# Wide half-precision products with no reader, set among the float32 products of a recurrence

## The chip, the cores and the metric

The kernel runs on one core of a Trainium2 chip. The metric is the time of one execution on the device, in microseconds. A core has a matrix engine (TensorE, PE in the profile, with its weight loads listed apart as PEld), a vector engine (VectorE, DVE), a scalar engine (ScalarE, ACT), GpSimd (POOL) and SyncE (SP), which here issues most of the transfers. Each works through its own list of instructions in order, and they wait for one another by semaphores. TensorE reads its operands from the on-chip memory and writes sums to PSUM, which has eight banks per partition; one bank holds 512 float32 values per partition.

## The reference

The reference is one layer of a hybrid decoder. A prompt of 2048 tokens and eight short samples of 8 tokens go through one input projection; its columns feed four groups of heads: attention, a gated linear recurrence, an RWKV-7 recurrence and a diagonal state-space model. Their outputs are joined, gated, projected by `w_out`, normalized and added to the input. What matters here is the RWKV-7 group, whose state goes from token to token, and the output projection:

```python
def step(S, inp):
    r_t, w_t, k_t, v_t, kk_t, a_t = inp
    sa = jnp.einsum('bhij,bhj->bhi', S, -kk_t)
    S = (S * w_t[:, :, None, :] + sa[..., None] * (kk_t * a_t)[:, :, None, :]
         + v_t[..., None] * k_t[:, :, None, :])
    return S, jnp.einsum('bhij,bhj->bhi', S, r_t)
...
y = x + rms_norm(jnp.einsum('bte,ed->btd', o, w_out), norm_post)
```

## The kernel before

The first 1180 us or so are projections, attention, the linear recurrence and the state-space model; the change does not touch them. Then comes the last phase, in `program` from line 1865 on: the RWKV-7 recurrence over sixteen blocks of 128 tokens (`rw_prompt`), the recurrence of the samples beside it (`rw_sample`), and the output projection tile by tile (`out_prep`, `out_tile`).

A block goes through these steps. `rw_prep` makes its vectors. `rw_mats` makes its matrices, on PSUM tiles named ra. `rw_base` solves the 16 by 16 diagonal pieces for two blocks at once: fifteen products of the tile r_de into ra, and then thirty short steps on VectorE (lines 1280 and 1281), in which each step needs the one before. `rw_tri` joins the pieces to the inverse of 64 by 64 (tiles r_XY, r_M, r_H, r_NA, on PSUM tiles rl). `rw_chain` carries the state through two chunks (tiles r_gs, r_Z, r_BK, r_ET, on PSUM tiles rc), and `rw_norm` normalizes. All these products are in float32, mostly 64 or 128 columns wide, and go through the small class `Marked` (`self.PE`), which hands them to TensorE and notes them in a list `done` that nothing reads. `front(i + 3)` runs up to three blocks ahead of the chain.

`out_tile` is the output projection of a tile of 128 tokens: two groups (g) of 24 float16 products of 512 columns each, the weights of the product being a piece of the tile's activations (o_h) and the moving operand a piece of `w_out` held as float16 (the tile wo, loaded once, lines 1537 and 1538). A group sums in one PSUM tile named acc; `ACB = 2` gives acc two banks, so that the next group may start while ScalarE (line 1612) still reads the one before. Products of `out_tile` are tied behind certain products of the chain (`spine`), so that they come among them.

The order on each engine is not written by hand: a scheduler of the framework puts the instructions in order by its own estimate of when each can run, within the bounds of the data and of `issue_after`, which keeps an instruction behind another on its engine. So a product that is added can also move the others.

Of the kernel before, what the change touches and what calls it, by code (L numbers as in the profile page):

```python
# [13 lines left out]
F32 = mybir.dt.float32  # L14
# [9 lines left out]
P = 128  # L24
# [12 lines left out]
class Marked:  # L37


    def __init__(self, eng):  # L40
        self.eng, self.done = eng, []

    def matmul(self, *a, **k):
        r = self.eng.matmul(*a, **k)  # L44
        self.done.append(r.ins)
        return r

    def transpose(self, *a, **k):
        r = self.eng.transpose(*a, **k)
        self.done.append(r.ins)  # L50
        return r


class Part:


    def __init__(self, ctx, tc, ins, outs):
        self.ctx, self.tc, self.nc = ctx, tc, tc.nc
        self.i, self.o = ins, outs
        nc = self.nc  # L60
        self.PE = Marked(nc.tensor)
        self.cst = ctx.enter_context(tc.tile_pool(name="cst", bufs=1))
        self.dram = ctx.enter_context(tc.tile_pool(name="scr", bufs=1, space=DRAM))
        self.od = [self.dram.tile([P, KT, n], F32, name=f"od{b}") for b, (_, n) in enumerate(BLK)]
        self.opool, self.gated, self.prep, self.wos = None, {}, {}, True
        self.onext = self.npiece = self.rwi = 0
        self.ident = self.cst.tile([P, P], F32, name="ident")
        make_identity(nc, self.ident)
        self.ones1 = self.cst.tile([1, P], F32, name="ones1")
        nc.vector.memset(self.ones1, 1.0)  # L70
        self.onec = self.cst.tile([P, 1], F32, name="onec")
        nc.vector.memset(self.onec, 1.0)
        self.vec = self.cst.tile([P, NVEC], F32, name="vec")
        nc.sync.dma_start(self.vec, ins["vec"])
# [1517 lines left out]
    def out_tile(self, i, h, sc, pool, psum, spine=()):  # L1592
# [7 lines left out]
        for g in range(2):  # L1600
            sl = slice(512 * g, 512 * g + 512)
            a = psum.tile([P, 512], F32, name="acc", bufs=ACB)
            c = 0
# [175 lines left out]
def weave(gens):  # L1779

    gens = [[g, 0, n] for g, n in gens]
    while any(x[2] > 0 for x in gens):
        g = min(gens, key=lambda x: x[1] / abs(x[2]))
        step = next(g[0], 0)
        g[1] += 1 if step is None else step
        if step == 0:
            gens.remove(g)


def drain(gen):  # L1790
    for _ in gen:
        pass


def program(tc, ins, outs):
    with ExitStack() as ctx:
        p = Part(ctx, tc, ins, outs)
        pool = lambda st, name, **kw: st.enter_context(tc.tile_pool(name=name, bufs=1, reuse_waits="tile", **kw))
        nc = tc.nc
        p.attn_consts()  # L1800
        ph2 = ctx.enter_context(ExitStack())
        with ExitStack() as ph1:
            hp = pool(ph1, "hp", side="right")
            acc = p.pwp = pool(ph1, "acc", space=PSUM, side="right")

            def paced(cols, lead):
                pos = -lead
                p.anchors = []

                def after(n):  # L1810
                    nonlocal pos
                    pos += n
                    i = int(pos * len(p.anchors) / (cols + 1))
                    return p.anchors[min(i, len(p.anchors) - 1)] if pos > 0 else None

                return after

            kps = ctx.enter_context(ExitStack())
            kp, sac = pool(kps, "s5k"), pool(kps, "sac")
            with ExitStack() as va:  # L1820
                vp = pool(va, "vp")
                p.w16b, p.w32b = 8, W32B
                with ExitStack() as st:
                    wp, ps = pool(st, "wp"), pool(st, "stp", space=PSUM)
                    lps = pool(st, "lgp", space=PSUM, side="right")
                    sp = wp
                    lr = pool(st, "lr")
                    p.norm_consts(sp)
                    p.wqkv = {0: p.load_w(0, wp, True)}
                    p.norm_in(0, hp, sp, ps)  # L1830
                    x0, h0 = p.xt_dma, p.hfs[-1]
                    p.qkv_start(wp, vp)
                    for k, b in enumerate(BORD):
                        if k < 4:
                            p.norm_in(BORD[k + 1], hp, sp, ps)
                            x1, h1 = p.xt_dma, p.hfs[-1]
                        p.qk(b, sp, acc)
                        with tc.issue_after(x0), tc.issue_after(h0):
                            if k == 0:
                                p.lam_consts(sp, ps)  # L1840
                                p.lru_consts(sp, ps)
                                p.lru_start(lr)
                            if k == 1:
                                p.proj_dram()
                                p.s5_consts(kp, sp)
                            if b == 4:
                                p.sample_consts(sac)
                        if k or LV:
                            p.lru(b, lr, lps, acc)
                        p.vtokens(b, sp, acc)  # L1850
                        if k == 0 and not LV:
                            p.lru(b, lr, lps, acc)
                        x0, h0 = x1, h1
                p.w16b, p.w32b = W16B, W32C
                ev, wp = pool(ph1, "ev", side="right"), pool(ph1, "wp2", side="right")
                aside = p.wo_steps(wp)
                with ExitStack() as st:
                    at, ps = pool(st, "at"), pool(st, "atp", space=PSUM)
                    after = paced(len(FILL) * 2 * TT, LEAD)
                    drain(p.attn_prompt(at, ps))  # L1860
                    drain(p.proj_rest(FILL, wp, ev, acc, after, aside))
        with kps, ExitStack() as st:
            sp, ps = pool(st, "sa"), pool(st, "sap", space=PSUM)
            weave([(p.attn_sample(sp, ps), SW), (p.s5(pool(st, "s5"), pool(st, "xps", space=PSUM)), S5N)])
        with ph2:
            rw, p.late = pool(ph2, "rw", side="right"), pool(ph2, "rwl", side="right")
            p.rps, p.rpb = pool(ph2, "rp", space=PSUM, side="right"), {"ra": 2, "rl": 2, "rc": 2}
            op = pool(ph2, "op")
            with ExitStack() as st:
                p.rwkv_consts(rw)  # L1870
                seq = p.rw_prompt(rw)
                weave([(p.s5_glu(pool(st, "s5g"), pool(st, "xg", space=PSUM)), 8), (islice(seq, 2 + 4 * RB), RBW)])
            ops = pool(ph2, "ops", space=PSUM)
            p.out_consts(op)
            p.opool = pool(ph2, "ot")
            sm = pool(ph2, "sm")
            p.rwkv_sample_consts(sm)
            smp = p.rw_sample(rw, sm)

            def out(t, spine=()):  # L1880
                if t not in p.prep:
                    p.out_prep(t)
                if GA and t + 1 < 15 and t + 1 not in p.gated and t + 1 not in p.prep:
                    p.out_gate(t + 1)
                p.out_tile(t, *p.prep.pop(t), p.opool, ops, spine)

            t = 0
            for i in range(RB, 16):
                mark = len(p.spine)
                n = min(-((t - 14) // (16 - i)), i - LAG - t)  # L1890
                for k in range(4):
                    next(seq, 0)
                    if k in SK:
                        next(smp, 0)
                    if n > 0 and k in POSL:
                        out(t, p.spine[mark:])
                        t, n, mark = t + 1, n - 1, len(p.spine)
                    if i == 15 and k == TK:
                        p.out_prep(16)
                while n > 0:  # L1900
                    out(t)
                    t, n = t + 1, n - 1
            while t < 15:
                out(t)
                t += 1
            out(16)
            out(15)
# [49 lines left out]
GYB = (4, 3)  # L1957
S5N = 20
KVB = 12
ACB = 2  # L1960
HALF = [(h, slice(64 * h, 64 * h + 64)) for h in range(2)]
QE = 0
X0E = 'gpsimd'
# [41 lines left out]
```

## Time and profile before

| | us |
|---|---|
| median of 3 runs | 1865.0 |
| lowest and highest run | 1857.7 and 1865.93 |
| profiled execution, its own time | 1853.69 |
| span of that execution, first to last instruction | 1851.9 |
| TensorE busy | 1520.3 (82% of the span) |
| VectorE busy | 1435.0 (77%) |
| ScalarE busy | 911.6 (49%) |
| GpSimd busy | 828.1 (45%) |
| mean granted clock of TensorE | 0.883 of full speed |

The granted clock (PEclk) is 1.00 at 2.4 GHz and 0.50 at 1.2 GHz; a value between them is a mean over a stretch with both. In the page's row of it, forty slices of 46.3 us each, it is 9 (0.9 or more) in most of the first 27 slices and between 5 and 9 in the last 13, which are the phase of the recurrence. A float32 product is recorded as two passes, so eight such products of the program are sixteen in the trace. The shown duration of a product contains its way through the array; how much of TensorE's time it takes is the distance to the start of the next.

### The profile page before, as it was taken

The numbers are of one execution on the slowest core, as the hardware profiler recorded it, in microseconds if no ns is written. First come the engines' busy times: TensorE is split into PE (matmuls) and PEld (weight loads), VectorE is DVE, ScalarE is ACT, GpSimd is POOL, SyncE is SP. The second block draws the span as 40 slices with busy tenths as digits, with TensorE's granted clock in tenths as the row PEclk, the third lists the DMA queues.
The fourth block names the chain that finished last, engine by engine and source line by source line (L and its number), as shares of the span: only waits on it lengthen the run. The fifth ranks groups of instructions, "written<-read, shape, count | busy, mean of one in ns | idle before, by whom it ended". The sixth has DMA issues, their size and how long they took to land.

```text
span 1851.9 us, 33637 instructions
## 1 busy us (share of the span) xinstructions
PE 1520.3 (82%) x11260; PEld 887.7 (48%) x11260; DVE 1435.0 (77%) x4320; ACT 911.6 (49%) x2229; POOL 828.1 (45%) x888
## 2 busy tenths in 40 slices
PE   4889878887888889788985899669788788888877
PEld 2445644444444444344443455447455455455543
DVE  7896549987899899789886763586777877877755
ACT  3545656554666567567761222343344444434433
POOL 3441226746578876353444452551333333433312
PEclk9999989998999999899996999775688878868979
DMA  4432134666354845563458877632112322212112
GB/s 148 132 95 81 41 115 120 141 130 139 91 129 107 199 119 141 136 145 92 89 108 257 247 224 249 207 111 82 45 50 84 88 56 86 89 55 72 54 48 70
DMA packets 294097, 216.17 MB, mean 117 GB/s; under 512 B 187778, under 2 KB 243812, under 8 KB 293412
## 3 DMA queue, kind: packets, MB, share of 16 engines
q1 hardware_dynamic: 281588, 175.66, 35.4%
q10 hardware_dynamic: 8496, 24.76, 4.6%
q0 software_dynamic: 3840, 13.61, 2.6%
q8 instruction: 89, 1.46, 0.3%
q14 instruction: 84, 0.69, 0.1%
HBM read 121.38 MB, written 52.70 MB: 94 GB/s over the span
## 4 chain that ended last, share of the span: by engine, by line
PE 33%; DVE 29%; DMA 8%; issue 7%; POOL 5%; ACT 4%; SPq 1%; ACTq 0%; POOLq 0%; DVEq 0%
PE acc L1608 7%; PE acc L206 6%; PE ra L44 4%; DVE a_mx L365 4%; DMA a_wt<-a_w 4%; DVE a_e L389 4%; PE rc L44 3%; DVE a_w L395 2%; PE ss L511 2%; DMA o_o<-od 2%; PE rl L44 2%; PE pf L530 1%; DVE r_W L1179 1%; POOL a_e L388 1%; DMA w<-in_w_in 1%
## 5 line engine op out<-in xcount | busy, mean ns | idle before, releaser
L206 PE MATMUL acc<-hT,w 128*128 128x512 f16 (+1 forms) x3120 | 633.2, 353 | 23.9 <-DVE qkhl L252 4.4
L206 PEld LDWEIGHTS <-w 128*128 128x128 f16 x3120 | 268.6, 100 | 318.0 <-issue 63.5
L368 ACT ACTIVATE a_e<-s,a_mx,sig 128x512 f32<-128x512 f32 (+3 forms) x320 | 227.0, 715 | 115.6 <-DVE a_mx L366 98.5
L1608 PE MATMUL acc<-wo,o_h 128*128 128x512 f16 (+1 forms) x816 | 209.8, 400 | 0.7 <-ACT o_y L1612 0.7
L365 DVE TENSOR_REDUCE a_mx<-s 128x1 f32<-128x512 f32 (+3 forms) x320 | 186.6, 600 | 21.7 <-PE s L361 13.8
L388 POOL TENSOR_SCALAR a_e<-a_e,a_al 128x512 f32<-128x512 f32 (+3 forms) x160 | 114.9, 734 | 148.9 <-DVE a_al L384 120.4
L389 DVE SCALAR_TENSOR_TENSOR a_e<-a_e,a_al 128x512 f32<-128x512 f32 (+3 forms) x160 | 148.8, 944 | 9.1 <-POOL a_e L388 9.0
L361 PE MATMUL s<-kh,qh 128*128 128x512 f16 (+3 forms) x320 | 106.4, 361 | 32.4 <-ACT a_e L368 29.0
L402 PE MATMUL pv<-vtok,a_wt 128*128 128x128 f16 x544 | 69.6, 229 | 67.6 <-DMA a_wt<-a_w 59.1
L392 ACT CAST a_w<-a_e 128x512 f16<-128x512 f32 (+3 forms) x160 | 86.3, 557 | 72.3 <-DVE a_e L389 65.4
L395 POOL TENSOR_TENSOR a_w<-a_e,a_w 128x512 f16<-128x512 f32 (+3 forms) x80 | 91.5, 1146 | 59.6 <-ACT a_w L392 59.6
L1608 PEld LDWEIGHTS <-o_h 128*128 128x128 f16 (+1 forms) x816 | 74.1, 102 | 85.8 <-issue 14.6
L402 PEld LDWEIGHTS <-a_wt 128*128 128x128 f16 x544 | 52.0, 103 | 92.1 <-DMA a_wt<-a_w 77.1
L1623 POOL TENSOR_TENSOR o_x<-o_y,o_x 128x512 f32<-128x512 f32 (+1 forms) x33 | 48.5, 1492 | 79.3 <-issue 64.1
L395 DVE TENSOR_TENSOR a_w<-a_e,a_w 128x512 f16<-128x512 f32 (+2 forms) x80 | 79.4, 995 | 2.5 <-ACT a_w L392 2.5
L1383 POOL TENSOR_TENSOR r_sd<-r_Z,r_Dp 64x128 f32<-64x128 f32 x64 | 35.5, 555 | 97.7 <-DVE r_Z L1391 94.5
L170 POOL TENSOR_TENSOR hT<-hf,hT 128x512 f16<-128x512 f32 (+1 forms) x36 | 36.7, 1025 | 86.1 <-ACT hT L168 83.6
L403 PE MATMUL pv<-vtok,a_wt 128*128 128x64 f16 x544 | 65.5, 201 | 0.0
L368 ACT ACTIVATION_READ_ACCUMULATOR a_e<-s,a_mx,sig 128x1 f32 x320 | 63.9, 200 | 0.0
L366 DVE TENSOR_SCALAR a_mx<-a_mx,sig 128x1 f32<-128x1 f32 x320 | 59.9, 202 | 0.4
L403 PEld LDWEIGHTS <-a_wt 128*128 128x128 f16 x544 | 50.7, 102 | 14.8 <-issue 7.9
L44 PE MATMUL ra<-r_W,r_F 64*128 64x128 f32 x256 | 37.7, 362 | 22.6 <-DVE r_F L1182 21.3
(553 smaller groups left out, 3498.9 us busy)
## 6 DMA issues: line engine op xcount, KB each, us to landing
kv<-in_ckv SPq DMA_DIRECT2D x128, 256.0 KB, 4.8
w<-in_w_in ACTq DMA_DIRECT2D x20, 512.0 KB, 3.7
pc<-pst SPq DMA_DIRECT2D x40, 256.0 KB, 2.3
xw<-in_xT SPq DMA_DIRECT2D x16, 512.0 KB, 4.2
w<-in_w_out ACTq DMA_DIRECT2D x16, 512.0 KB, 4.3
sg<-pst SPq DMA_DIRECT2D x32, 256.0 KB, 2.2
r_X<-pc SPq DMA_DIRECT2D x16, 512.0 KB, 3.8
o_x<-in_x SPq DMA_DIRECT2D x16, 512.0 KB, 3.6
```

Source lines behind the costliest of these rows:

```text
L44: r = self.eng.matmul(*a, **k)
L206: self.nc.tensor.matmul(acc[:, :n], w16[:, k, a, :], h[:, k, e, :], start=(c == 0), stop=(c == 3 * KT - 1))
L361: ins = nc.tensor.matmul(s[:, :kn], q[:, c], kh[:, c, k0:k0 + kn], start=True, stop=True)
L365: nc.vector.tensor_reduce(mx[:, p, c:c + 1], s[:, :kn], axis=AX.X, op=ALU.max, negate=True)
L368: nc.scalar.activation(e[:, :kn], s[:, :kn], AF.Exp, scale=sig, bias=mx[:, p, c:c + 1], accum_out=l[:, p, c:c + 1])
L388: nc.gpsimd.tensor_scalar(e1[:, :kn], e1[:, :kn], al[:, p, 1:2], 0.0, op0=ALU.mult, op1=ALU.add)
L389: nc.vector.scalar_tensor_tensor(e0[:, :kn], e0[:, :kn], al[:, p, 0:1], e1[:, :kn], op0=ALU.mult, op1=ALU.add)
L392: nc.scalar.copy(w[:, :kn], e0[:, :kn])
L395: eng.tensor_tensor(w[:, kn:], e0[:, :kn], w[:, :kn], op=ALU.subtract)
L402: ins = nc.tensor.matmul(pv[:, :P], wt[:, j], v, start=kt == 0, stop=kt == qb, skip_group_check=True)
L403: nc.tensor.matmul(pv[:, :64], wt[:, nt + j], v[:, :64], start=False, stop=kt == qb, skip_group_check=True)
L1608: nc.tensor.matmul(a[:n].rearrange("p (c n) -> p c n", c=4), h[:, k, e], self.wo[:, 4 * g:4 * g + 4, k, f, :], start=c == 0, stop=c == 3 * ...
```

## The change

`Marked` no longer keeps a list. It counts the columns of the products and transposes that go through it. Once they reach `WIDE = 280` it issues one more product directly behind the last (by `issue_after`) and starts to count anew. That product has a 128 by 128 piece of wo as its weights and four such pieces as its moving operand, so 512 columns in float16, and writes to a PSUM tile named junk, which nothing reads. This is switched on where the loop over the blocks begins. The junk tile takes a bank of PSUM, and `ACB` goes from 2 to 1 to make room for it.

```diff
 class Marked:
-    def __init__(self, eng):
-        self.eng, self.done = eng, []
-
-    def matmul(self, *a, **k):
-        r = self.eng.matmul(*a, **k)
-        self.done.append(r.ins)
+    def __init__(self, eng, tc):
+        self.eng, self.tc, self.wide, self.cols = eng, tc, None, 0
+
+    def issued(self, r, out):
+        self.cols += math.prod(out.shape[1:])
+        if self.wide and self.cols >= WIDE:
+            self.cols = 0
+            junk, a = self.wide
+            with self.tc.issue_after(r.ins):
+                self.eng.matmul(junk, a[:, 0], a, start=True, stop=True)
         return r
...
+    def matmul(self, out, *a, **k):
+        return self.issued(self.eng.matmul(out, *a, **k), out)
+
+    def transpose(self, out, *a, **k):
+        return self.issued(self.eng.transpose(out, *a, **k), out)
...
-        self.PE = Marked(nc.tensor)
+        self.PE = Marked(nc.tensor, tc)
...
+            p.PE.wide = ops.tile([P, 4, P], F32, name="junk"), p.wo[:, 0:4, 0, 0, :]
             t = 0
             for i in range(RB, 16):
...
-ACB = 2
+ACB = 1
+WIDE = 280
```

In the order of TensorE the changed program has 378 such products, each with its weight load. 45 stand ahead of the first base solve inside the loop, 57 in the first pair of blocks behind it, 48 in each of the next five pairs, and 36 in the last. Of the 48 of a pair, 21 stand alone between other products and 27 in runs of ten, seven, four, four and two.

The start of the loop on TensorE, before (r_XY, r_M and r_H belong to `rw_tri` of the first block, the ra rows to the blocks ahead of it and to the samples):

```order
L44 MATMUL ra<-r_W,r_F 128x128 x8
L44 MATMUL rl<-r_XY,r_M 64x64 x8
L49 MATMUL ra<-ident,r_Fd 128x128 x4
L44 MATMUL ra<-r_prk,selh 64x128 x4
L44 MATMUL rl<-r_XY,r_H 64x64 x8
L49 MATMUL ra<-ident,r_xv 128x128 x2
```

And the same place now, where `Marked`'s lines are L53 and L56 instead of L44 and L49, and L49 is the added product:

```order
L53 MATMUL ra<-r_W,r_F 128x128 x8
L53 MATMUL rl<-r_XY,r_M 64x64
L49 LDWEIGHTS wo
L49 MATMUL junk<-wo 128x512
L53 MATMUL rl<-r_XY,r_M 64x64 x5
L49 LDWEIGHTS wo
L49 MATMUL junk<-wo 128x512
L53 MATMUL rl<-r_XY,r_M 64x64 x2
L56 MATMUL ra<-ident,r_Fd 128x128 x4
```

The other products keep their places there; the added ones are cut in between.

TensorE behind a base solve of the steady part, before (the row of r_de is the last of its fifteen products; the products of r_XY and r_M need the solved pieces):

```order
L44 MATMUL ra<-r_de_17448,rwrow 128x32
L44 MATMUL ra<-r_X,rw_15071 32x128 x4
L44 MATMUL ra<-r_L,rw_15073 128x128 x2
L44 MATMUL ra<-hsel,r_sq 128x2 x2
L44 MATMUL ra<-r_L,rw_15073 128x128 x2
L116 MATMUL ra<-ident,r_rs 64x128 x4
L44 MATMUL ra<-r_W,r_F 128x128 x8
L44 MATMUL rl<-r_XY,r_M 64x64 x8
```

That is so behind every second base solve; behind the others products of the chain and of acc stood in that place before as well. Now, behind each of the steady ones (L1613 is the product of `out_tile`, fifteen of them in a row at this place, of which the first stands here):

```order
L53 MATMUL ra<-r_de_17567,rwrow 128x32
L49 LDWEIGHTS wo
L49 MATMUL junk<-wo 128x512
L49 LDWEIGHTS wo
L49 MATMUL junk<-wo 128x512
L49 LDWEIGHTS wo
L49 MATMUL junk<-wo 128x512
L49 LDWEIGHTS wo
L49 MATMUL junk<-wo 128x512
L1581 MATMUL rl<-o_mx,onec 128x1
L49 LDWEIGHTS wo
L49 MATMUL junk<-wo 128x512
```

```order
L53 MATMUL rc<-r_gs,r_TT 64x64
L49 LDWEIGHTS wo
L49 MATMUL junk<-wo 128x512
L53 MATMUL rc<-r_gs,r_TT 64x64 x3
L1613 LDWEIGHTS o_h
L1613 MATMUL acc<-wo,o_h 128x512
```

So the products of the chain and of acc have moved to a place behind every base solve, where they stood behind every second one, and the added products stand in a run ahead of them.

## Rows read from the trace of the kernel before

**Rows 1.** The page's totals by engine, and its row of the granted clock.

```profile
PE 1520.3 (82%) x11260; PEld 887.7 (48%) x11260; DVE 1435.0 (77%) x4320; ACT 911.6 (49%) x2229; POOL 828.1 (45%) x888
PEclk9999989998999999899996999775688878868979
```

**Rows 2.** Windows of all engines: stretch, its length, busy times, clock, DMA.

```profile
core 0: us, PE busy (x) PEld busy (x) DVE busy (x) ACT busy (x) POOL busy (x), PEclk, DMA share, GB/s
1270.00:1300.00 30.00, 29.55 (x252) 26.05 (x252) 16.11 (x72) 8.58 (x29) 2.67 (x7) 0.50 0.11 28
1413.00:1555.00 142.00, 118.54 (x1094) 77.24 (x1094) 111.31 (x379) 62.31 (x172) 52.74 (x69) 0.82 0.26 75
```

**Rows 3.** Windows of PE alone: length, busy time, clock, DMA.

```profile
1250.00:1313.00 63.00, 54.84 (x473) 0.50 0.25 73
1332.00:1356.00 24.00, 14.36 (x102) 0.52 0.09 23
1410.00:1423.00 13.00, 9.52 (x74) 0.61 0.25 81
1450.00:1457.00 7.00, 4.06 (x29) 0.53 0.41 112
1477.00:1506.00 29.00, 18.72 (x149) 0.51 0.22 64
```

**Rows 4.** Windows of line 1608 alone (acc products): PE, PEld, clock, DMA.

```profile
1250.00:1300.00 50.00, 0.00 (x0) 0.00 (x0) 0.50 0.26 76
1500.00:1550.00 50.00, 24.39 (x96) 8.23 (x96) 0.91 0.23 68
```

**Rows 5.** The chain that ended last, 1250 to 1313 us, its shares by line.

```profile
by line: PE ra L44 25.1%; PE rc L44 23.4%; PE rl L44 11.3%; issue 4.2%; DVE o_o L1552 2.9%; PE ra L49 2.6%; DVE r_prk L1171 2.3%; DVE r_W L1210 2.1%; DVE r_cum L1143 2.0%; DVE o_h L1586 2.0%; DVE r_x L1281 1.9%; DVE r_SM__16357 L1405 1.8%; 
```

**Rows 6.** Timeline of PE: start, us, product, count of passes, idle time before.

```profile
1404.55 0.68 PE L44 MATMUL rl<-r_XY,r_M 64*64 64x64 f32 x16
1405.16 1.69 PE L1608 MATMUL acc<-wo,o_h 128*128 128x512 f16 x7
1406.78 0.68 PE L44 MATMUL rl<-r_XY,r_H 64*64 64x64 f32 x16
...
1425.72 0.39 PE L1608 MATMUL acc<-wo,o_h 128*128 128x512 f16 x1
1425.95 0.38 PE L49 MATMUL ra<-ident,r_xv 128*128 128x128 f32 x2
1426.16 3.19 PE L1608 MATMUL acc<-wo,o_h 128*128 128x512 f16 x14
1429.28 0.62 PE L44 MATMUL ra<-r_X,rw 128*32 128x128 f32 x6
...
1468.49 1.62 PE L44 MATMUL ra<-r_de,rwrow 128*128 128x120 f32 x14
...
1482.33 1.12 PE L116 MATMUL ra<-ident,r_rs 128*64 128x128 f32 x8 [5.60 <-DVE r_rs L111]
1487.01 3.09 PE L44 MATMUL ra<-r_W,r_F 64*128 64x128 f32 x16 [3.57 <-DVE r_F L1182]
...
1516.31 1.49 PE L44 MATMUL ra<-r_W,r_F 64*128 64x128 f32 x16
...
1527.48 1.63 PE L44 MATMUL ra<-r_de,rwrow 128*128 128x120 f32 x14
```

**Rows 7.** Timeline of PE and ACT near the end, two groups of acc.

```profile
1807.85 5.34 PE L1608 MATMUL acc<-wo,o_h 128*128 128x512 f16 x24 [0.39 <-ACT o_y L1612]
1813.03 0.50 PE L1576 MATMUL rl<-o_mx,onec 128*128 128x1 f32 x4
1813.29 0.69 ACT L1612 ACTIVATE o_y<-acc,o_sc 128x512 f32<-128x512 f32 x1 [2.52 <-PE acc L1608]
```

**Rows 8.** The loads of wo: issue durations, first and last issue, landing.

```profile
L1538 SPq DMA_DIRECT2D wo<-wod x8: 333/431/487, 1176.8 to 1180.2; - x8
DMA to landing us min/median/max: 3.6/5.7/9.1
```

More of the change, by code (lines that the diff above doesn't have):

```diff
@@ L37 @@
 class Marked:
-    def __init__(self, eng):
-        self.eng, self.done = eng, []
-    def matmul(self, *a, **k):
-        r = self.eng.matmul(*a, **k)
-        self.done.append(r.ins)
-        return r
[L48 to L51, printed above, removed]
+    def __init__(self, eng, tc):
[7 more added lines that the diff above has]
+                self.eng.matmul(junk, a[:, 0], a, start=True, stop=True)
+        return r
+    def matmul(self, out, *a, **k):
+        return self.issued(self.eng.matmul(out, *a, **k), out)
+    def transpose(self, out, *a, **k):
+        return self.issued(self.eng.transpose(out, *a, **k), out)
 class Part:
```

## Prediction

> **What bounds the kernel now.** I read the page's totals and its row of the clock first [rows 1]: TensorE is the busiest engine with 82% of the span, VectorE has 77%, and the clock is near full for the first two thirds and well below in the last. Then windows of the last phase. Two pairs of blocks, 1413 to 1555 us, take 142 us, so 71 us a pair; in them TensorE is busy 118.5 us and VectorE 111.3 us [rows 2]. A pair thus has 59.3 us of TensorE and 11.7 us in which it stands idle, and no engine is full.
>
> The clock tells where TensorE's time is long without need. In five stretches the granted clock is 0.50 to 0.61, so nearly all of them ran at 1.2 GHz, and TensorE was busy in them for 54.8, 14.4, 9.5, 4.1 and 18.7 us [rows 3]. It isn't idleness alone: from 1270 to 1300 us it was busy 29.55 of 30 us at 0.50 [rows 2]. What differs is the kind of product. From 1250 to 1300 us no product of line 1608 runs and the clock is 0.50; from 1500 to 1550 us there are 96 and it is 0.91 [rows 4]. The price of the low clock is plain in one pair of rows: the same sixteen passes into ra took 3.09 us at 1487 us and 1.49 us at 1516 us [rows 6].
>
> **What the change adds.** 378 products of 512 columns. At full speed fourteen products of the same width take 3.12 us, from 1426.16 to 1429.28, so 0.22 each; one that stands alone among products of 128 rows takes 0.23 (1425.72 to 1425.95). Between products of 64 rows seven take 1.62 us (1405.16 to 1406.78), which is 0.08 more than seven times 0.22, so one alone would be 0.30 [rows 6]. At the low clock I bound one by twice the first price, 0.44. I take 0.23 for those that stand alone, the nearest row, and 0.22 for those in runs. In all that is 84 us of TensorE; 166 us is the upper bound, were all of them at the low clock. What they wait for is wo, which was issued by 1180.2 us and landed within 9.1 us [rows 8], long before the first of them near 1254 us, and the junk bank, which only TensorE writes. So they add no wait of their own.
>
> **What it takes away: the low clock.** In the steady part I count, for two pairs, the low share of each stretch, which is (1 minus clock) over 0.5: 0.78 of 9.5 us, 0.94 of 4.1 and 0.98 of 18.7, together 29.6 us [rows 3]. At full speed that is half, so 14.8 us less for two pairs and 7.4 a pair: 59.3 becomes 51.9. The added products fill a pair with 21 alone (4.8 us) and 27 in runs (5.9 us). The runs stand where the scheduler saw TensorE wait, in the base solve above all, and there it does wait: 5.60 and 3.57 us in a row behind one of them [rows 6]. I let them all lie in the 11.7 us of idle time, of which 5.8 stay. Sum of a pair: 51.9 + 4.8 + 5.9 + 5.8 = 68.4 us against 71, 2.6 us less. From 1356 to 1800 us there are 6.25 such pairs: **16 us less**. The bounds of this term: 71 us can fall to 63.8, below, and rise to 78.7 (both under the rivals).
>
> The Trainium skill has a rule that speaks against single products set in so: "TensorE: Matmul & The Clock Gate", Part 3, "What overlaps and what doesn't", says that a weight load runs under products in flight only when it is for another group of rows. A full-height weight load between products of 64 rows would then lie bare. The rows just read, 0.08 us over seven products, do not bear that out; the result by the rule is the fifth rival.
>
> **The start, 1250 to 1356 us.** In the first 63 us, all at the low clock, 62.4% of the chain that ended last is TensorE (25.1 + 23.4 + 11.3 + 2.6, [rows 5]), 39 us. At full speed it is 19.7 us less; I give 3 us back because the clock has to rise first. 45 added products go in here, by my count of the order 25 alone (5.8 us) and 20 in runs; of the runs' 4.4 us half lies in waits and 2.2 on the chain. VectorE does not take over, with 16.1 of 30 us busy [rows 2]. That is 19.7 - 3 - 5.8 - 2.2 = 8.7 less, and from 1332 to 1356 us, where TensorE is busy 14.4 of 24 us and mostly follows VectorE, 1.3 us more: **10 us less**. Bounds: nothing, and 20.
>
> **One bank for acc.** The next group can now start only when ScalarE has read the last one, 0.69 us from 1813.29 on, where with two banks the next had its turn at once [rows 7]. In the steady part seven or more products of the chain stand between two groups, about 1 us, which covers it. Behind the last block there are six changes of group with next to nothing between them: 6 times 0.69, **4 us more**. If the cover fails everywhere, 33 changes cost 23 us. In one place two banks already made TensorE wait 0.39 us for ScalarE [rows 7].
>
> **Sum.** 16 + 10 - 4 = 22 us less. The profiled execution took 1853.7 us, so 1831.7; the median of the runs shown is 11.3 us above that execution, so the forecast is **1843 us**. About 0.5%, 9 us, is what a measurement of this kernel can tell from no change.
>
> **Rivals.** First, *the runs lie in the way*. The scheduler placed them by its own estimate, and TensorE takes its list in order: a run of ten in front of the last base products delays them by 2.2 us whether or not the chip waits there, and VectorE's solve with them. Then nothing is hidden: 51.9 + 10.7 + 11.7 = 74.3 us a pair, 3.3 more, 21 us in 6.25 pairs; the start gives 6.5, the tail costs 4. That is 18 more, or 1883 us. It decides from the point where fewer than 15 of the 27 products in runs (3.3 of 5.9 us) fall into idle time. For it: TensorE has hardly idle time in the stretches at full clock, and its load of 62.6 us a pair would be more than the 59.3 of now. Against it: the idle time in the base solve is there [rows 6].
>
> Second, *VectorE keeps the pace*. It is busy 55.7 us of a pair, its own list is in order, and thirty steps of a base solve depend on each other. Then a pair stays at 71, the start gives 10, the tail costs 4: 6 less, 1859 us. For it: both long waits of [rows 6] are for VectorE. Against it: it is idle for 15 us of a pair.
>
> Third, *the new order is worth more than the clock*. Before, only every second base solve had products of the chain and of acc behind it; now each of the steady ones has. From the base products at 1468.49 to those at 1527.48 us, a pair with that cover, it was 59.0 us [rows 6], and so 83 for the other. If all went like the first, with 4.8 us of single products on top, a pair takes 63.8: 7.2 less, 45 in all, with the start and the tail 51 less, 1814 us. Against it: VectorE would be busy 87% of that.
>
> Fourth, *the clock does not rise*, and the change does not do what it could. Then a pair is 59.3 + 10.7 + 2.9 (half of them at 0.44 in place of their hidden share) + 5.8 = 78.7, 48 more; in the start 45 at 0.44 are 20, of which 7 lie in waits, so 13 more, and the tail 4: 1930 us. Against it: the clock is up wherever products of 512 columns come often [rows 4], and in the start one stands behind every 280 columns.
>
> Fifth, *weight loads lie bare*. A load for line 1608 is 8.23 us over 96, 0.09 [rows 4]; over all products of the steady part it is 77.24 over 1094 passes, so 0.14 for the two passes of a float32 product [rows 2]. If an added product lays its own load and the next one bare, a single one costs 0.23 more: 4.8 a pair, which makes 73.2, 14 more in 6.25 pairs; the start then gives 4 and the tail costs 4: 14 more, 1879 us. Against it: the 0.08 us over seven products [rows 6].
>
> **Chances.** The forecast 0.42, the runs in the way 0.22, VectorE's pace 0.14, the new order 0.12, the bare loads 0.05, the clock that stays 0.05. The likeliest one's own range is 1826 to 1862: below, the start is worth 20 and a fourth of the single products is hidden too (7 us); above, the changes of acc cost 23 in place of 4. The range over the cases goes from 1814 to 1893: the third rival is in, and the first with ten more for acc, while the fourth is left out. Faster by over 0.5% are 0.33 of the forecast's 0.42, the new order and 0.05 of VectorE's pace, 0.50. Within 0.5% are 0.08 of the forecast, 0.08 of VectorE's pace and 0.02 of the runs, 0.18. Slower are 0.01 of each of the first two of these, 0.20 of the runs and the last two, 0.32.
>
> **What would show it.** Right: the clock from 1260 to 1310 us near 1.00 and the sixteen passes into ra near 1.5 us there; no stretch like 1477 to 1506 us in the steady part; base products about 68 us apart; junk products in runs with TensorE's waits for VectorE shorter around them. Wrong: pairs at 74 us with the clock full, products waiting in TensorE's list behind runs while VectorE and ScalarE wait for them; or a clock of 0.5 in spite of the added products; or waits of acc for line 1612 in the steady part.

## The result, and the profile after

The changed kernel takes 1914.0 us (median of 4 runs, 1900.5 to 1918.0) where the kernel before takes 1861.4 beside it (1857.1 to 1865.9): a ratio of 1.028, 95% interval 1.022 to 1.034. It is 52 us slower; the forecast was 22 us faster, with a range that ended at 1893. The profiled execution took 1900.5 us, the fastest of them, so differences read from its trace come out smaller than those of the medians.

The page's totals and its row of the clock answer to [rows 1]. TensorE has 90 us more, VectorE none, and the clock's row has lost its lowest digits but is not full in the last third.

```profile
PE 1610.8 (85%) x11638; PEld 919.3 (48%) x11638; DVE 1427.2 (75%) x4320; ACT 910.3 (48%) x2229; POOL 815.9 (43%) x888
PEclk9999989998999999899979998766898898998989
```

Windows of all engines, with the columns of [rows 2]: the start, then two pairs of blocks, from the base products of one to those of the next but one.

```profile
1270.00:1300.00 30.00, 28.07 (x306) 20.12 (x304) 18.11 (x76) 9.36 (x32) 5.04 (x12) 0.84 0.11 28
1474.81:1625.52 150.71, 140.28 (x1181) 84.67 (x1180) 110.01 (x378) 61.89 (x173) 49.03 (x68) 0.93 0.23 71
```

A pair takes 75.4 us where it took 71; TensorE is busy for 70.1 of them (59.3 before), idle for 5.2 (11.7 before). Its time has filled the idle time and gone past it. Windows of TensorE alone show where the clock is still low (length, busy time, clock, DMA), to be held against [rows 3].

```profile
1250.00:1270.00 20.00, 19.36 (x140) 0.50 0.46 140
1290.00:1330.00 40.00, 35.97 (x222) 0.57 0.17 53
1346.00:1364.00 18.00, 13.90 (x102) 0.53 0.12 32
1502.00:1514.00 12.00, 9.63 (x63) 0.58 0.37 115
1580.00:1590.00 10.00, 9.39 (x64) 0.54 0.29 107
```

There is still a stretch in every pair, of 10 to 12 us; before, every second pair had one of 29. The chain of waits from 1474 to 1550 us, its shares by line, says what the added products cost there: 14.4% of 76 us is 10.9 us a pair, where the forecast had 4.8 and the rest in idle time.

```profile
by line: PE junk L49 14.4%; PE ra L53 13.2%; PE acc L1613 12.5%; PE rc L53 7.5%; PE rl L53 4.7%; DMA o_o<-od 4.5%; issue 3.1%; DVE r_W L1184 2.2%; PE ra L56 2.1%; DVE oq L114 2.0%; DVE o_y L1626 1.7%; DVE r_W L1215 1.7%; DVE o_h L1591 1.7%;
```

The timeline of TensorE (start, us, product, count, idle time before) shows two of the ways in which they lie there: a run of ten in the middle of the base products, and one alone in the middle of four products into rc, which are eight passes (the counts of the timeline are passes, two for a float32 product).

```profile
1474.81 1.62 PE L53 MATMUL ra<-r_de,rwrow 128*128 128x120 f32 x14
...
1476.90 2.32 PE L49 MATMUL junk<-wo 128*128 128x512 f16 x10
1479.05 0.57 PE L53 MATMUL ra<-r_de,rwrow 128*128 128x88 f32 x4
...
1490.92 0.44 PE L53 MATMUL rc<-r_Z,r_ET 64*64 64x64 f32 x6
1491.30 0.39 PE L49 MATMUL junk<-wo 128*128 128x512 f16 x1
1491.62 0.32 PE L53 MATMUL rc<-r_Z,r_ET 64*64 64x64 f32 x2
1491.87 0.82 PE L1613 MATMUL acc<-wo,o_h 128*128 128x512 f16 x3
```

From 1490.92 to 1491.87 are 0.95 us. The same eight passes without the added one take 0.38 (below). The 0.57 between them is the number the prediction lacked.

Behind the last block the groups of acc now start 6.17 us apart, with a wait of 0.83 us for ScalarE between them where 0.69 was priced:

```profile
1869.61 5.34 PE L1613 MATMUL acc<-wo,o_h 128*64 128x512 f16 x24 [0.83 <-ACT o_y L1617]
1875.78 5.34 PE L1613 MATMUL acc<-wo,o_h 128*128 128x512 f16 x24 [0.83 <-ACT o_y L1617]
```

### The profile page after: what moved, and what is told of

Its sections match the earlier page's. It is cut to its first block, busy times and chain, and to the rows that moved or that the text cites. A ratio compares the mean times of both kernels' runs of the same rounds, so it can differ in the third digit from the quotient of the medians.

```text
span 1898.7 us, 34360 instructions
## 1 busy us (share of the span) xinstructions
PE 1610.8 (85%) x11638; PEld 919.3 (48%) x11638; DVE 1427.2 (75%) x4320; ACT 910.3 (48%) x2229; POOL 815.9 (43%) x888
## 4 chain that ended last, share of the span: by engine, by line
PE 38%; DVE 25%; issue 8%; DMA 6%; POOL 5%; ACT 4%; SPq 1%; ACTq 0%; POOLq 0%; DVEq 0%
PE acc L1613 7%; PE acc L211 5%; PE junk L49 5%; PE ra L53 5%; DVE a_mx L370 4%; PE rc L53 3%; DVE a_e L394 3%; DMA a_wt<-a_w 3%; PE rl L53 2%; DVE a_w L400 2%; PE ss L516 2%; PE pf L535 1%; POOL a_e L393 1%; POOL a_w L400 1%; DVE a_mx L371 1%
## 5 line engine op out<-in xcount | busy, mean ns | idle before, releaser
L1613 PE MATMUL acc<-wo,o_h 128*128 128x512 f16 (+1 forms) x816 | 196.0, 383 | 4.2 <-ACT o_y L1617 4.2
L49 PE MATMUL junk<-wo 128*128 128x512 f16 x378 | 131.6, 428 | 0.0
L1613 PEld LDWEIGHTS <-o_h 128*128 128x128 f16 (+1 forms) x816 | 74.1, 99 | 85.7 <-issue 6.8
L1388 POOL TENSOR_TENSOR r_sd<-r_Z,r_Dp 64x128 f32<-64x128 f32 x64 | 27.9, 437 | 159.9 <-DVE r_Z L1396 156.8
L407 PEld LDWEIGHTS <-a_wt 128*128 128x128 f16 x544 | 52.0, 103 | 91.5 <-DMA a_wt<-a_w 75.9
L53 PE MATMUL ra<-r_W,r_F 64*128 64x128 f32 x256 | 41.1, 373 | 28.2 <-DVE r_F L1187 28.2
```

Of the source, the lines that this page charges most:

```text
L49: self.eng.matmul(junk, a[:, 0], a, start=True, stop=True)
L53: return self.issued(self.eng.matmul(out, *a, **k), out)
L407: ins = nc.tensor.matmul(pv[:, :P], wt[:, j], v, start=kt == 0, stop=kt == qb, skip_group_check=True)
L1613: nc.tensor.matmul(a[:n].rearrange("p (c n) -> p c n", c=4), h[:, k, e], self.wo[:, 4 * g:4 * g + 4, k, f, :], start=c == 0, stop=c == 3 * ...
```

## The experiments

Differences between kernels below are differences of their ratios to the kernel before, each measured beside it, times 1861 us.

### First: parts of the change, each ordered anew by the scheduler

**One bank alone** (no products):

```
-WIDE = 280
+WIDE = 10 ** 9
```

> The changed kernel without any added product: acc keeps its one bank. Theory A (the added products lie on the chain): 1861 plus 5 to 8 us for the groups of acc that follow each other at the end, so 1864 to 1872. Theory B (the one bank and the order that comes with it cost the time): 1895 to 1915, as the changed kernel. Theory C (the runs lie in the way): as A.

Measured: 1857.7 us, ratio 0.998 (0.995 to 1.000). One bank for acc costs nothing in all, though the tail shows its waits. Theory B is out.

**Narrow products**, 32 columns in place of 512:

```
-                self.eng.matmul(junk, a[:, 0], a, start=True, stop=True)
+                self.eng.matmul(junk[:, 0, :32], a[:, 0], a[:, 0, :32], start=True, stop=True)
```

> All 378 added products, but 32 columns wide in place of 512, at nearly the changed kernel's places in the order. They take some 0.05 us each and should leave the clock as low as before. Theory A: the one-bank kernel's time plus 378 times 0.05 to 0.08, so 1885 to 1900, with the clock of the recurrence near 0.80. Theory B: 1895 to 1915 as well, but then the kernel with one bank alone is there too. Theory C: near 1875, since a run of ten is then 0.5 us long.

Measured: 1915.0 us, ratio 1.028 (1.026 to 1.030), the loss of the wide ones to within the interval; theories A and C had less. So a product's own width is not all of its price. The trace gives the first hint of the rest: a narrow product holds TensorE for 0.12 us (1506.47 to 1506.59), but the eight passes into rc that it splits take 0.75 us, from 1506.10 to 1506.85, not 0.38.

```profile
1506.10 0.44 PE L53 MATMUL rc<-r_Z,r_ET 64*64 64x64 f32 x6
1506.47 0.19 PE L49 MATMUL junk<-wo 128*128 128x32 f16 x1
1506.59 0.33 PE L53 MATMUL rc<-r_Z,r_ET 64*64 64x64 f32 x2
1506.85 0.82 PE L1613 MATMUL acc<-wo,o_h 128*128 128x512 f16 x3
```

That is still 0.2 less than the 0.57 of a wide one. The clock makes up for it: from 1250 to 1850 us it is 0.76, where the wide ones have 0.88 and the order alone (below) 0.82. So narrow ones don't raise it, and the equal loss is a sum of two differences, not one price.

**Only the 166 that stood alone**, then **half of all** (one for every 560 columns, 215):

```
+            self.n += 1
+            if self.n - 1 not in KEEP:   # KEEP: the 166 that stood alone in the changed kernel
+                return r
```

> Only the 166 added products that stood alone in the changed order; the 212 in runs are left out. Theory A: each costs 0.3 us on the chain, 50 us, and gives back most of the clock's 63 us where it comes up: 1850 to 1880, some 35 us below the changed kernel. Theory C (only the runs cost): below the kernel before, 1830 to 1850. Theory B: 1890 or more.

```
-WIDE = 280
+WIDE = 560
```

> WIDE = 560: 215 added products, of which 103 stand in runs. Theory A: cost by count, 215 times 0.25 to 0.3 against 378, so 40 to 50 us less of it, and the clock a little lower: 1870 to 1890. Theory C: by the share of the runs, about half of them gone, 1875 to 1890. Theory B: 1895 or more.

Measured: 1909.0 us, ratio 1.027 (1.023 to 1.031), and 1893.3 us, ratio 1.020 (1.015 to 1.024). The first is above theories A and C and the second between A and B; only B's bounds hold the first, and one bank alone had put B out. Neither parts what is left: the scheduler gave each kernel an order of its own, and I took the new order, not the products, for a good share of the loss. The next runs hold the order fixed.

### Second: order and products apart

From here on the order in which a scheduler put one kernel's instructions on every engine is read off and written down as edges of issue order, so that another kernel keeps it:

```
+    for n in order:                      # a scheduled order, as places in the traced program
+        i = mine[n]
+        behind(tc, i, last.get(i.engine))    # a NoSync edge to the one before on its engine
+        last[i.engine] = i
```

**The changed kernel's order without its products:**

> The instructions of every engine stand exactly as in the changed kernel, but its 378 wide products are left out. Theory O (the order that came with the products costs most of it): 1885 to 1895 us, pairs of blocks still 73 us apart or more. Theory P (the products' own time in TensorE's way costs it, the order nothing): 1854 to 1862 us, as the kernel with one bank and no products (1857.7). Between the two, the share of the 56 us between 1857.7 and 1914.0 is read off.

Measured: 1856.3 us, ratio 0.996 (0.995 to 0.998). Theory O, which I held by then, is out: order and bank together gain 7 us, and three steady pairs are 68.4 us apart on the mean (base products at 1469.34 and 1674.49). Against one bank alone the order gains 3, which can't be told from nothing. All of the loss is the products. Here are the eight passes of the last fence in this kernel, 0.38 us from 1386.16 to 1386.54:

```profile
1386.16 0.45 PE L56 MATMUL rc<-r_Z,r_ET 64*64 64x64 f32 x8
1386.54 0.82 PE L1616 MATMUL acc<-wo,o_h 128*128 128x512 f16 x3
```

**The order of the kernel with one bank, with the products put in**, each alone right behind the product that calls for it (362; then one for every 560 columns, 199; then for every 1120, 104):

```
+        if i.name in JUNK[1]:            # i calls for a wide product
+            j = next(junk)
+            behind(tc, j, i)
+            last[i.engine] = j
```

> The order of the kernel with one bank and no products is kept on every engine, and 362 wide products are put into it, each alone behind a product of the recurrence (no runs; the first 16 of 378 are left out). Theory O: 1865 to 1880 us, since the order is the good one. Theory P: 362 x 0.32 us less what idle time and a faster clock give back, 1900 to 1925 us. Theory R (only the runs of 4 to 17 cost): 1850 to 1862 us, since there are none.

> The same with a wide product for every 560 columns, 199 of them. Theory P: half of what e7 lost against 1857.7, less or more by the clock: 1875 to 1890 us. Theory O and R: 1855 to 1870 us. If the clock is already near 1.0 with half the products, it is below half of e7's loss.

> The same with a wide product for every 1120 columns, 104 of them. Theory P: a quarter of e7's loss, 1865 to 1875 us, if the clock rises in the same measure as the products are set; below 1857 us only if the clock rises with far fewer products than their price does. Theory O and R: 1852 to 1865 us.

Measured: 1990.1 us, ratio 1.069 (1.066 to 1.071); 1916.1 us, 1.030 (1.026 to 1.034); 1898.8 us, 1.018 (1.016 to 1.021). Against one bank alone that is 132, 60 and 38 us, or 0.36, 0.30 and 0.37 us a product. All three are higher than any theory had them, and the price does not fall with fewer: the clock of 1250 to 1850 us is 0.84 with 362 and 0.80 with 104, against 0.81 with none. The timeline of the first:

```profile
1501.28 0.34 PE L53 MATMUL rc<-r_Z,r_BK 128*64 128x64 f32 x4
1501.55 0.39 PE L1918 MATMUL junk<-wo 128*128 128x512 f16 x1
1501.87 0.34 PE L53 MATMUL rc<-r_Z,r_BK 128*64 128x64 f32 x4
1502.14 1.47 PE L1613 MATMUL acc<-wo,o_h 128*128 128x512 f16 x6
```

Four passes take 0.27 us, the added one 0.32, four more 0.27: 0.86 for eight passes that took 0.38. Half as many in a row don't take half the time, so a group that is cut in two loses 0.16, and the product in the cut takes 0.32 where one between groups can take 0.23. Of the 362 some 250 stand inside a group.

The single products in five traces with a fixed order (these three, e11_between and e15_singles_alone) and in the changed kernel can be compared so with the same place without them, where the clock is full and no wait is near. What a product adds goes by the weights of its two neighbours, given as rows by columns. Between neighbours of the same small shape (64 by 64, 128 by 64, 64 by 128, 32 by 32 or 128 by 32) it is 0.44 to 0.57 us by shape, 0.51 in the median of 311 places, nearly all of them inside a group. Between two small shapes that differ it is 0.32 (91 places). With weights of 128 by 128 on one side or both it is 0.22 or less, inside such a group too (16 places). So the cut by itself costs nothing; it costs where both neighbours share a shape and the added product has another.

**The same 362, held back until the group is through:**

```
+            while due and what != was:       # what: operands and result of the product that comes
+                j = next(junk)
+                behind(tc, j, last[i.engine])
```

> As e7_own_order, with its 362 wide products, but each is held back until the group of products that it would cut in two is through (249 alone, 46 pairs, 7 threes). Theory S (a product costs 0.22 us between groups, and 0.5 us where it splits a group of products of 32 or 64 rows, which run side by side): 1895 to 1925 us. Theory B (each lays weight loads bare wherever it stands): as e7, 1975 to 1995 us.

Measured: 1899.6 us, ratio 1.019 (1.015 to 1.024). The same number of products, most of them moved by a few places, costs 92 us less. Theory S holds, and theory B, one price wherever a product stands, is out. A product between groups takes 0.23 us ahead of a full product of acc, the prediction's price, and 0.32 between two small shapes that differ (here r_X, 128 by 32, which stands ahead of it, and r_TT):

```profile
1523.42 0.39 PE L1918 MATMUL junk<-wo 128*128 128x512 f16 x1
1523.74 0.44 PE L53 MATMUL rl<-r_TT,r_H 32*32 32x32 f32 x16
...
1526.58 0.39 PE L1918 MATMUL junk<-wo 128*128 128x512 f16 x1
1526.81 0.81 PE L1613 MATMUL acc<-wo,o_h 128*128 128x512 f16 x3
```

**Runs and single ones of the changed kernel**, in its own order, each kind at its places (GAPS holds the place and the count):

```
+        if pe and n in GAPS:
+            for _ in range(GAPS[n]):
+                j = next(junk)
+                behind(tc, j, last[i.engine])
+                last[i.engine] = j
```

> The order of the changed kernel on every engine, with only the 212 wide products that stand there in runs of 2 to 17, at their places. Theory S (single ones that split a group cost most): 1856 to 1872 us, a third or less of the 58 us between 1856.3 (order alone) and 1914.0. Theory R (the runs are in the way): 1885 to 1905 us, most of it.

> The order of the changed kernel, with only the 166 wide products that stand alone there, at their places. Theory S: 1890 to 1912 us. Theory R: 1860 to 1880 us. If the two parts add up, this and e14_runs_alone lie together some 58 us above twice 1856.3; if less, the clock that one part gives helps the other.

Measured: 1874.3 us, ratio 1.011 (1.005 to 1.016), and 1889.9 us, 1.017 (1.013 to 1.021). Against the order alone the 212 in runs cost 26 us and the 166 single ones 38, each give or take some 10. Both theories are half right. The sum, 65, is 6 over the 59 that all cost together, which is less than the intervals; whether the clock that one part gives helps the other stays open.

### Third: the clock, and products in idle time

In the trace of the order alone, windows of TensorE show when the clock falls (length, busy time, clock; the last two are a closer look at the fall):

```profile
1478.00:1484.00 6.00, 6.00 (x61) 1.00 0.24 70
1484.00:1490.00 6.00, 4.14 (x39) 1.00 0.23 66
1490.00:1496.00 6.00, 1.41 (x20) 0.51 0.18 44
1496.00:1508.00 12.00, 10.76 (x78) 0.50 0.40 131
1514.00:1554.00 40.00, 37.78 (x358) 1.00 0.25 72
...
1489.00:1490.00 1.00, 0.55 (x8) 1.00 0.00 0
1490.00:1491.00 1.00, 0.67 (x14) 0.54 0.00 0
```

It falls near 1490.1 us, behind a wait of 1.86 us, and stays low for 20 us, through a second wait of 4.26 us and the work behind it. Both waits are for VectorE, once a pair:

```profile
1489.45 0.66 PE L124 MATMUL ra<-ident,r_rs 128*64 128x128 f32 x8 [1.86 <-DVE r_rs L119]
1490.44 1.12 PE L56 MATMUL rl<-r_XY,r_H 64*64 64x64 f32 x16 [0.33 <-ACT r_H L1320]
1495.81 3.09 PE L56 MATMUL ra<-r_W,r_F 64*128 64x128 f32 x16 [4.26 <-DVE r_F L1190]
```

So wide products were put there and nowhere else: 185 in the 18 idle stretches of 1.2 us or more, filling some three quarters of each; and the same with products of 32 columns.

```
+GAPS = {6234: 9, 6238: 9, ..., 7230: 6, 7242: 15, 7557: 6, 7569: 14, ...}
```

> The instructions stand as in e6_order_alone, and 185 wide products are put where its trace shows TensorE idle for 1.2 us or more, in runs ahead of the product that waits there, some 75% of each idle stretch by 0.22 us a product (45% of the first two, at the low clock). Theory I (the clock falls because TensorE stood idle just before, and a product in idle time costs nothing): the clock stays at 1.00 in the steady part, the pairs of blocks come down from 68.3 us to 61 to 65, and the time to 1815 to 1840 us. Theory K (the clock follows the kind of product, not idle time, as the prediction had it): 1852 to 1862 us with the low stretches as before. Theory R (any run is in the way of what waits): over 1865 us.

> As e10_idle, at the same places and in the same number, but the added products have 32 columns, so TensorE stays idle for most of each stretch. Theory I: the clock falls as in e6_order_alone and the time is 1850 to 1862 us. If the presence of an fp16 product is enough, whatever its width: as e10_idle.

Measured: 1850.9 us, ratio 0.994 (0.991 to 0.998), and 1850.3 us, 0.994 (0.992 to 0.997). Neither can be told from the order alone (0.996), so products in idle time cost nothing that can be measured, but they brought nothing yet. With the narrow ones the clock is what it is in the order alone, 0.82 from 1250 to 1850 us, with falls at the same waits; the wide ones make it 0.86. An fp16 product of any width is thus not enough. That does not part its width from the time that it fills, since the narrow ones leave TensorE idle. The timeline of the wide ones says why they brought nothing:

```profile
1489.49 3.41 PE L1921 MATMUL junk<-wo 128*128 128x512 f16 x15
1493.65 1.71 PE L56 MATMUL ra<-r_W,r_F 64*128 64x128 f32 x16 [0.74 <-DVE r_F L1190]
1495.29 0.44 PE L56 MATMUL rl<-r_X,r_NA 32*32 32x32 f32 x16
1496.37 0.64 PE L56 MATMUL rl<-r_TT,r_H 32*32 32x32 f32 x16 [0.64 <-ACT r_H L1331]
1499.17 1.09 PE L59 MATMUL ra<-ident,r_Fd 128*128 128x128 f32 x4 [2.17 <-POOL o_x L1631]
```

The sixteen passes into ra now take 1.64 us and not 3.02, and soon TensorE waits 2.17 us for GpSimd (0.61 in the order alone). The clock falls after all, but at 1496.0 us, a microsecond before this long wait begins. Ahead of the fall TensorE was busy for 4.99 of 6 us; it lies in the wait of 0.64 us for ScalarE, behind one of 0.74:

```profile
1490.00:1496.00 6.00, 4.99 (x46) 1.00 0.33 89
1496.00:1500.00 4.00, 1.46 (x20) 0.50 0.02 7
1500.00:1510.00 10.00, 10.00 (x64) 0.52 0.45 141
```

So theory I fails twice, in its time and in its reason: long waits are not the only thing behind which the clock falls. From 1400 to 1800 us of this trace it falls eleven times, mostly behind waits of under 1 us. The changed kernel shows it without any wait (windows of its trace):

```profile
1288.00:1292.00 4.00, 4.00 (x34) 1.00 0.15 33
1292.40:1309.20 16.80, 16.80 (x97) 0.50 0.11 33
```

There TensorE had just run thirty passes of base products, of 2 to 30 columns each, without a pause. What such passes and idle time have in common for the clock these runs do not show.

**The waits that are left filled too**, 81 products more, and then 31 more:

```
-GAPS = {6234: 9, 6238: 9, ..., 7242: 15, 7557: 6, 7569: 14, ...}
+GAPS = {6234: 16, 6238: 13, ..., 7242: 15, 7258: 2, 7266: 7, 7557: 6, 7569: 14, 7585: 2, 7593: 8, ...}
```

> As e10_idle, with 81 more wide products where its own trace still shows TensorE idle, above all 7 or 8 ahead of the transposes that waited 2.17 to 2.35 us for GpSimd's o_x, behind which the clock fell to 0.50 for 14 us of each pair; 266 in all. Theory I1 (TensorE's time at the low clock still sets the pair): the last low stretch goes, pairs from 68.9 to 61 to 65 us, time 1810 to 1835 us. Theory I2 (VectorE's and GpSimd's chain sets the pair, and TensorE only waits longer for it): clock near 1.00 throughout, pairs 66 to 69 us, time 1840 to 1855 us, the waits for r_F, r_rs or o_x longer by what TensorE became faster. Theory R: the added runs delay what waits behind them, over 1858 us.

> As e13_idle_twice with 31 more wide products in the stretches in which its trace shows TensorE idle before a low clock, 297 in all. Theory I: 1830 to 1841 us, since the low stretches at 1350, 1430, 1630 and 1755 us shrink and the one from 1274 to 1313 may. If VectorE and GpSimd set the pace by now: 1838 to 1845 us, no change.

Measured: 1840.9 us, ratio 0.989 (0.985 to 0.992), and 1839.3 us, 0.989 (0.985 to 0.993). Both beat the kernel before and the changed one. In the first the clock holds through the stretch, and its three steady pairs are 66.4 us apart on the mean (1463.70 to 1662.89), against 68.4 in the order alone:

```profile
1490.00:1496.00 6.00, 4.95 (x60) 1.00 0.21 62
1496.00:1500.00 4.00, 3.27 (x28) 1.00 0.47 167
1500.00:1510.00 10.00, 10.00 (x116) 1.00 0.43 127
...
1274.00:1310.00 36.00, 33.23 (x293) 0.50 0.13 34
```

Theory I1 hoped for 61 to 65 us: the clock's gain of some 7 us a pair became 2, since VectorE's chain comes next (I2, at the lower end of what it gave). Over those three pairs VectorE holds 60% of the chain that ended last and TensorE 24%, where it is 46% and 39% in the order alone; GpSimd, which I2 named beside VectorE, has none of it. The third fill brings no more that can be measured. The low clock of the start stays in both.

## Why the prediction was wrong

**The steady term failed, at three of its four numbers.** It made a pair 51.9 + 4.8 + 5.9 + 5.8 = 68.4 us; it takes 75.4.

*The single products, 4.8 us.* The price of 0.23 was read in a row of [rows 6] with weights of 128 by 128 behind it. At such places it holds, as e11_between shows. The change counts columns, and drops its product wherever the count is full, which is between neighbours of the same small shape for 101 of the 166 that stand alone. There it is 0.51. From 1475 to 1776 us, four pairs, 50 stand so, 4 between small shapes that differ and 28 beside 128 by 128: (50 x 0.51 + 4 x 0.32 + 28 x 0.22) / 4 = 8.2 us a pair. I had asked about this, as a weight load that lies bare, and answered it with the 0.08 us over seven products of acc. But 0.08 is only what the seven take more themselves, as the one in the cut above takes 0.32 in place of 0.23; what the passes around it lose, 0.16 there, that row can't show.

The fifth rival, drawn from the Trainium skill ("TensorE: Matmul & The Clock Gate", Part 3, "What overlaps and what doesn't"), priced a single product at 0.46 and got the mean near, with a chance of 0.05. The traces are mixed: between neighbours of the same small shape they agree in size (0.44 to 0.57), beside weights of 128 by 128 they do not (0.22). Whether it is a bare load, the end of side-by-side work of small products or the change of shape itself was not parted by a run; that a product of 32 columns adds as much beside its own time as one of 512 (0.25 in the two fences above) fits all three.

*The runs, 5.9 us hidden.* They lie on the chain. The first rival was right in kind: the ten at 1476.90 stand before base products that wait for nothing, and the 212 cost 26 us where I had them at nothing but 2.2 us in the start. In the order alone TensorE goes on with those base products, at 1471.22, with no idle time before them. The long wait that stays, 3.79 us for r_F (below), has none of the added products in front.

*The clock, 7.4 us given back.* The low share of busy time in two pairs was 29.6 us; it is 8.1 + 8.6 by the two windows above, so 3.2 us a pair came back. I had argued from 1270 to 1300 us that it isn't idleness alone, since TensorE was busy there at 0.50, and from [rows 4] that the kind of product makes the difference. That is true as far as it goes: at the start the clock stays low under products of the recurrence for 36 us or more, before and still in e13_idle_twice (two of its 293 passes there are added ones), and in the changed kernel it fell at 1292 us with no idle time. But from 1400 to 1800 us of the kernel before, the changed one and the order alone, 22 of 23 low stretches start in or behind a wait of over 1.5 us. In [rows 6] the wait of 5.60 us stands at the head of the stretch 1477 to 1506, and I read it only as room for the runs. The Trainium skill has this in the page named above, under "Why this matters for your kernels": idle gaps between products are what loses the full clock. The falls behind the waits of 1.86 us (e6_order_alone) and 3.79 us (below) agree, the falls at 1496.0 us in e10_idle and at 1292 us in the changed kernel do not. The change put no product into the long gaps, since each follows a product of the recurrence and there is none in a gap; its own trace has one 3.79 us long, behind which the clock falls, with no added product in it:

```profile
1503.76 2.99 PE L53 MATMUL ra<-r_W,r_F 64*128 64x128 f32 x16 [3.79 <-DVE r_F L1187]
```

**The start, -10 us**, did not come. From base products at 1233.94 us to those at 1334.68 are 100.7 us, where they were 94.4 (1234.48 to 1328.86), so the start became 6 us longer, outside the term's bounds of nothing to 20 less. Behind the run of eleven at 1266.61 us the clock rose to 1.00 for some 20 us (0.84 from 1270 to 1300 us, where it was 0.50), but 5.2 us after the run began, where I had given 3 without a row for it, and the run took 4.8 us itself; from 1290 to 1330 us the clock was down again. The same stretch takes 93.5 us in the order alone, 97.4 with the single products and 101.4 with the runs, so both cost time here, the runs more.

**One bank, +4 us**, is right where it was put: 6.17 us from group to group in the tail, where 5.2 had been from 1807.85 to 1813.03 [rows 7]. In the steady part there is one wait for it, of 0.2 us, and over the whole kernel it costs nothing that can be measured (e1_one_bank).

**The new order**, which the third rival made worth 51 us, is worth 7 together with the bank. **VectorE's pace**, the second rival, does not decide in the changed kernel, where TensorE has 64% of the chain from 1474.81 to 1625.52 us and VectorE 26%; it comes to decide once TensorE is faster (e13_idle_twice).

Altogether, of the 52 us: order and bank -7, runs +26, single ones +38, and 6 too many, which is inside the intervals. The prediction's own sum with what the trace shows is 4.4 us more in 6.25 pairs, 6 in the start and 4 in the tail, 38 us; the two profiled executions are 47 apart, and the other 9 I can't place.

## What to carry to other kernels

Price an added instruction at the very place where it will stand: the same product cost 0.22 us beside products of its own shape, 0.5 between small ones that share a shape, and nothing that could be measured in a wait. Before adding work to keep a clock up, find what the engine did just before the clock fell; where that is a wait, work belongs into it, and each wait that is filled shows what sets the pace next. An order that a scheduler gives can be held fixed, and then a change in the order and the added work are two numbers and not one.

## What the runs showed of the hardware

An fp16 product with weights of 128 by 128 adds 0.51 us between float32 products that share a smaller shape, 0.32 between smaller shapes that differ, and 0.22 beside a product of 128 by 128. A narrow one adds as much to a group that it splits, beside its own time, as a wide one. The clock did not rise with narrow ones (0.76), and with single wide ones behind every 1120 columns neither (0.80, against 0.81 with none). It fell from 1.00 near 1292.3 us in the changed kernel, where TensorE had been busy for 4.00 of 4 us. And the 20 us of low clock in a pair of the order alone, with some 15 us of TensorE's work in them, could shrink to 3 to 7 without the pair getting 7 us shorter: it got 2 shorter, and VectorE's share of the chain rose from 46% to 60%.
